# Moving the making of the Hyena filters from the second mixer to the end of the first

## The chip, the cores and the metric

The kernel runs on one core of one Trainium2 chip. The metric is the device time of one execution in microseconds (us); a row gives the median of several runs, or the one execution that the profiler recorded. TensorE (PE) does matmuls and transposes, VectorE (DVE), ScalarE (ACT) and GpSimd (POOL) do the rest, and SyncE (SP) issues most DMAs. GpSimd issues the others from its own instruction stream.

## The reference

Two layers of a model over 128 context tokens and 512 latent tokens, of width 1024. Layer 0 has a mixer of scans (S5 and RG-LRU), layer 1 a mixer with a long convolution (Hyena); after each mixer comes a layer of product-key experts (PEER).

```
def mixer_c(h, P, lo, grid):                       # layer 1
    z = h @ P['w_in_c'][lo] + P['b_in_c'][lo]      # 1024 -> 3 x 1024
    z = dwconv_rows(z, ...)
    x0, x1, v = split(z, 3)
    v = v * x1
    circ = hyena_filters(length, P['hy_w1'][lo], ..., P['hy_decay'][lo])
    v = bidir_long_conv(v, circ) + P['hy_bias'][lo] * v
    return (v * x0) @ P['w_out_c'][lo] + P['b_out_c'][lo]

def hyena_filters(length, w1, b1, f1, w2, b2, f2, w3, decay):
    z = sin(f1 * (emb @ w1 + b1))                  # positions only
    z = sin(f2 * (z @ w2 + b2))
    filt = (z @ w3).reshape(length, 2, HY_WIDTH)
    filt = filt * (exp(-t * abs(decay)) + HY_SHIFT)
    circ = concatenate([filt[:, 0], 0, filt[:0:-1, 1]])
    return circ * rsqrt(sum(circ * circ) + EPS)
```

What matters here: the filters hang on weights and positions alone, not on the activations. They can be made at any time before the long convolution of layer 1.

## The kernel before

All activations lie transposed (features on the 128 partitions, 640 tokens along them). The program runs four stages in turn: the first mixer (0 to about 452 us of the profile), the expert layer of layer 0, the second mixer (its input projections begin at about 2080 us), the expert layer of layer 1.

**Projections.** `proj3` (L164) multiplies one 128-column block of weights at a time. Each weight tile `wraw` comes by a DMA on SP into a ring of three buffers, ScalarE rounds it to `wh` (L159), GpSimd subtracts to get the rest `wl` (L77), and TensorE multiplies in three passes (L171): for a depth of 1024 that is 8 x 3 x 2 = 48 matmuls of 320 columns into `pproj`, for a depth of 512 it is 24. After each block `proj3` calls the function `evac` that it was given.

**The end of the first mixer.** `w_glu` gives 4 blocks of 24 matmuls, each followed by `evg` (a sigmoid on ScalarE, a product and a split on VectorE, into `mH`, `mL`). `w_out_ab` gives 8 blocks of 48 matmuls, each followed by `evo` (the addition to the residual stream `xT`, and its square for the next norm). Then `rms_rstd` sums the squares (`pssq`, L207) and broadcasts the norm by a matmul, `prs` (L225). The expert layer starts with that norm (`nt`, `hHg`, `hHd`), its transposes `phr`, and the query projections with `wq`.

**The second mixer's input projections.** `w_in_c` gives 24 blocks of 48 matmuls, each followed by `evc` (bias, a short convolution `zc` to `zo` on VectorE, and for every second block a product `vv` and five transposes `pva`, `pvb`). Then the convolution starts with a load of the kernel table `K`.

**The filters.** `filters(fp)` (L315) is a generator: each `next` issues one step, 43 in all.

- Two steps make the small network on 640 positions (matmul `pz`, reduction of the angle on VectorE, sine on ScalarE), into `zfin`.
- Then four chunks of 256 channels follow. A chunk loads `w3` and `dec` on SP, and does one small step for the context and four big steps for the latent tokens (k = 0 to 3). Each step is an exponential `f` (L350), the matmul `pf` (L353), their product (L95), a sum and a difference `pmf` (L77), a rounding to `pmpH`, `pmmH` (L360), subtractions to `pmpL`, `pmmL` on GpSimd, and a square; from the second big step on GpSimd adds the square to `sqa`.
- The chunk's tables are transformed with Fourier matrices `fc`, which GpSimd loads (L307, two buffers): six matmuls `pkf` for the context (L380), 48 for the latent tokens (L394). The results go to memory as `kf_dc` and `kf_ds` on SP. The sums of squares are reduced by `pss` (L372).
- The tiles `f`, `dec`, `sqa` and the four `PM` tiles have one buffer each, and `kfc`, the context's result, shares the tag and so the buffer of `f`:

```
                    kf = fp.tile([128, 2, CW], F32, name="kfc", tag="f", bufs=FBUF)
                    S.copy(kf, p)
                    nc.sync.dma_start(kf_d[0][:, :, c0:c0 + CW], kf)
```

Before the change, `mixer_c` takes FG0 = 6 steps ahead of the projections and FG1 = 3 in each `evc`, so all are issued by the 13th of the 24 blocks.

**What sets the order.** The code is written as a stream, but a scheduler places every instruction: it runs the program on a timeline of its own and puts on each engine whichever instruction is ready there. The order of each engine's instructions is then fixed, and an engine waits for the operand of its next instruction even when a later one could run. A tile waits for the readers of whatever lay in its memory before.

Of the kernel before, what the change touches and what calls it, by code (L numbers as in the profile page):

```python
# [43 lines left out]
def tile_kernel(ctx: ExitStack, tc: tile.TileContext, I, O, dbg=None, upto=99):  # L44
# [34 lines left out]
    def mul(o, a, b, eng=None):  # L79
        tt(o, a, b, ALU.mult, eng)  # L80

    def add(o, a, b, eng=None):
        tt(o, a, b, ALU.add, eng)
# [13 lines left out]
    def bc(a, shape):  # L97
        return a.to_broadcast(shape)
# [50 lines left out]
    def tick(n=1):  # L149
        for _ in range(n):  # L150
            if bgm[0] is None or next(bgm[0], False) is False:
                bgm[0] = None
                break
# [10 lines left out]
    def proj3(wsrc, nm, kk, segs, evac, pre=()):  # L164
        for m in range(nm):
            wh, wl = pre[m] if m < len(pre) else wsplit(wsrc[m])
            p = ps.tile([128, 2, 512], F32, name="pproj", tag="pp")
            for k in range(kk):
                for a, hl in ((wh, 0), (wh, 1), (wl, 0)):
                    for i, sg in enumerate(segs):  # L170
                        PE.matmul(p[:, i, :sg[2]], a[:, k, :], sg[hl](k), start=k == 0 and a is wh and hl == 0,  # L171
                                  stop=k == kk - 1 and a is wl)
            evac(m, p)

    def halves(H, L):
        def f(x, h):
            return lambda k: x[:, k, h * HALF:(h + 1) * HALF]
        return [(f(H, h), f(L, h), HALF) for h in range(2)]
# [23 lines left out]
    def rms_rstd(acc, pool, alloc, a=0, b=T, tag="", stag="sm"):  # L202
        n = (b - a) // 128
        p = ps.tile([128, 8], F32, name="pssq", tag=stag)
        add(acc[0], acc[0], acc[1])
        for i in range(n):
            PE.matmul(p[:, i:i + 1], acc[0][:, i * 128:(i + 1) * 128], ones[:, 0:1], start=True, stop=True)  # L207
        v, r, t = (pool.tile([128, 5], F32, name="nv" + c, tag="nv" + c + (tag or ""), bufs=1)[:, :n] for c in "abc")
        ts(v, p[:, :n], 1.0 / D, EPS, ALU.mult, ALU.add)
        S.activation(t, v, AF.Sqrt)  # L210
        V.reciprocal(r, t)
        mul(t, r, r)
        mul(t, t, v)
        ts(t, t, -0.5, 1.5, ALU.mult, ALU.add)
        mul(r, r, t)
        dg = alloc()[:, :b - a].rearrange("p (i c) -> p i c", c=128)
        sh = [128, n, 128]
        mul(dg, bc(ident.unsqueeze(1), sh), bc(r.unsqueeze(2), sh))
        if tag == "c":
            o = ps.tile([128, 512], F32, name="prs", tag="sm2")  # L220
        else:
            o = ps.tile([128, 2, 512], F32, name="prs", tag="pp").rearrange("p a b -> p (a b)")
        for i in range(0, n, 4):
            e = min(i + 4, n)
            PE.matmul(o[:, i * 128:e * 128], ones, dg[:, i:e].rearrange("p a b -> p (a b)"), start=True, stop=True)  # L225
        return o[:, :b - a]
# [44 lines left out]
    def resid(l, which, m, p):  # L271
        g = modT[l][:, which * 24 + 16 + m, :]
        for s, a, b in SEG:
            for h in range(2):
                lo, hi = max(a, h * HALF), min(b, (h + 1) * HALF)
                if lo < hi:
                    stt(xT[:, m, lo:hi], p[:, h, lo - h * HALF:hi - h * HALF], g[:, s:s + 1], xT[:, m, lo:hi],
                        ALU.mult, ALU.add)
# [30 lines left out]

    PASSES = ((0, 0), (0, 1), (1, 0))  # L310

    FBUF = 1
    PBUF = 2

    def filters(fp):  # L315
# [19 lines left out]
        for cc in range(D // CW):  # L335
# [8 lines left out]
            for sq_, ln, nk, tg in SEQS:  # L344
                PM = [[fp.tile([128, nk, CW], F32R, name=t, tag=t) for t in r] for r in PMT]
                sqa = fp.tile([128, 2, CW], F32, name="sqa", tag="sqa")
                for k in range(nk):
                    i = sq_ + k
                    f = fp.tile([128, 2, CW], F32, name="f", tag="f", bufs=FBUF)
                    S.activation(f, dec, AF.Exp, scale=tneg[:, i:i + 1])  # L350
# [24 lines left out]
                if sq_ == 0:  # L375
                    fc = fload(fp, "fc", I["fc_c"], 4)
                    p = ps.tile([128, 2, CW], F32, name="pkf", tag="sm2")
                    for ri in range(2):
                        for a, b in PASSES:
                            PE.matmul(p[:, ri], fc[:, ri * 2 + a], PM[ri][b][:, 0], start=(a, b) == (0, 0), stop=a == 1)  # L380
                    kf = fp.tile([128, 2, CW], F32, name="kfc", tag="f", bufs=FBUF)
                    S.copy(kf, p)
# [500 lines left out]
    with ExitStack() as ed:  # L883
        dp = ed.enter_context(tc.tile_pool(name="mxd", bufs=1))
        mH = dp.tile([128, 8, T], F32R, name="mH")
        mL = dp.tile([128, 8, T], F32R, name="mL")
        zH = dp.tile([128, 4, T], F32R, name="zH")
        zL = dp.tile([128, 4, T], F32R, name="zL")
        bg = vec("s5_b_glu")
        for j in range(4):  # L890
            split(zH[:, j], zL[:, j], zs[:, j])
            split(mH[:, 4 + j], mL[:, 4 + j], xg[:, j])

        tick(1000)

        def evg(m, p):
            t = dp.tile([128, T], F32, name="sg", tag="sg", bufs=2)
            S.activation(hv(t), pv(p), AF.Sigmoid, bias=bg[:, m:m + 1])
            mul(t, t, zs[:, m])
            split(mH[:, m], mL[:, m], t)  # L900

        proj3(I["w_glu"], 4, 4, halves(zH, zL), evg)
        def evo(m, p):
            resid(0, 0, m, p)
            one(m)

        acc, one = squares(lambda: dp.tile([128, T], F32, name="nsq", tag="nsq", bufs=6))
        proj3(I["w_out_ab"], 8, 8, halves(mH, mL), evo)
        rn[0] = rms_rstd(acc, dp, lambda: dp.tile([128, T], F32, name="nsq", tag="nsq", bufs=6))
    mx.close()  # L910
    dump("x1", xT)
# [10 lines left out]
    c_d = [dram.tile([ND, 128, 4, 2, 128], BF16, name=f"c_d{l}") for l in range(2)]  # L922
    g_d = [dram.tile([16, 128, TD // 16, 8, 16], F32, name=f"g_d{l}") for l in range(2)]

    FG0, FG1 = 6, 3
    ORD = (1, 2, 3, 4, 0)
    NGB = 5
    NGS = 3
# [482 lines left out]
    def mixer_c():  # L1411
# [4 lines left out]
        vH = mp.tile([128, 5, D], F32R, name="vH", tag="vmH")  # L1416
        vL = mp.tile([128, 5, D], F32R, name="vL", tag="vmL")
        bi, cw, cb = vec("b_in_c"), vec("hy_conv_w", 3, 24), vec("hy_conv_b")
        with ExitStack() as e0:
            ap, hH, hL = hc  # L1420
            fg = filters(e0.enter_context(tc.tile_pool(name="hyf", bufs=1)))
            order = [m for j in range(8) for m in (8 + j, 16 + j)] + list(range(8))
            pre = [wsplit(I["w_in_c"][m]) for m in order[:WPRE]]
            for _ in range(FG0):
                next(fg, None)
            x1 = [None]

            def evc(i, p):
                for _ in range(FG1):
                    next(fg, None)  # L1430
                m = order[i]
                z = ap.tile([128, T], F32, name="zc", tag="nrm", bufs=4)
                S.activation(hv(z), pv(p), AF.Identity, bias=bi[:, m:m + 1])
                o = ap.tile([128, T], F32, name="zo", tag="nrm", bufs=4)
                S.activation(o, z, AF.Identity, scale=cw[:, 1, m:m + 1], bias=cb[:, m:m + 1])
                ro, ri = (a.rearrange("p (r c) -> p r c", c=64) for a in (o, z))
                w0, w2 = cw[:, 0, m:m + 1], cw[:, 2, m:m + 1]
                stt(ro[:, :, 1:], ri[:, :, :63], w0, ro[:, :, 1:], ALU.mult, ALU.add)
                stt(ro[:, :, :63], ri[:, :, 1:], w2, ro[:, :, :63], ALU.mult, ALU.add)
                stt(o[:, 64:65], z[:, 63:64], w0, o[:, 64:65], ALU.mult, ALU.add)  # L1440
                stt(o[:, 63:64], z[:, 64:65], w2, o[:, 63:64], ALU.mult, ALU.add)
                if m < 8:
                    nc.sync.dma_start(x0_d[m], o)
                elif m < 16:
                    x1[0] = o
                else:
                    j = m - 16
                    mul(vv[:, j], o, x1[0], G)
                    pa = ps.tile([128, 4, 128], F32, name="pva", tag="sm")
                    pb = ps.tile([128, 4, 128], F32, name="pvb", tag="sm2")  # L1450
                    for i_ in range(5):
                        if i_ == 0:
                            tk = slice(0, TC)
                        else:
                            e, k = divmod(i_ - 1, 2)
                            tk = slice(TC + e + k * 256, TC + (k + 1) * 256, 2)
                        PE.transpose(pa[:, i_] if i_ < 4 else pb[:, 0], vv[:, j, tk], ident)
                    js = slice(j * 128, (j + 1) * 128)
                    S.copy(vH[:, 0:4, js], pa)
                    S.copy(vH[:, 4, js], pb[:, 0])  # L1460
                    sub(vL[:, 0:4, js], pa, vH[:, 0:4, js].bitcast(F32))
                    sub(vL[:, 4, js], pb[:, 0], vH[:, 4, js].bitcast(F32))

            proj3([I["w_in_c"][m] for m in order], 24, 8, halves(hH, hL), evc, pre)
            for _ in fg:
                pass
            e_c.close()
            bgm[0] = mods_ring(1, tuple(range(MQ, 10)))
        with ExitStack() as e1:
# [276 lines left out]
```

## Time and profile before

| | |
|---|---|
| median of 3 runs | 4136.21 us (4134.04 to 4140.57) |
| the profiled execution, its own time | 4135.69 us |
| its span, first to last instruction | 4133.9 us |
| mean granted TensorE clock, share of full speed | 0.938 |
| busy share of the span: PE, DVE, ACT, POOL | 87%, 82%, 40%, 55% |
| first mixer's gates and output projections | 373.1 to 452.2 us |
| second mixer's input projections, with the filters | 2079.8 to 2320.8 us |

Busy shares are averages over stages with different limits; a change is read from the stage that it touches. The chain that ended last is followed back from the last instruction to what released each step. The granted clock is a share of 2.4 GHz: 0.50 is 1.2 GHz, and values between are means over a stretch.

### The profile page before, as it was taken

The numbers are of one execution on the slowest core, as the hardware profiler recorded it, in microseconds if no ns is written. First come the engines' busy times: TensorE is split into PE (matmuls) and PEld (weight loads), VectorE is DVE, ScalarE is ACT, GpSimd is POOL, SyncE is SP. The second block draws the span as 40 slices with busy tenths as digits, with TensorE's granted clock in tenths as the row PEclk, the third lists the DMA queues.
The fourth block names the chain that finished last, engine by engine and source line by source line (L and its number), as shares of the span: only waits on it lengthen the run. The fifth ranks groups of instructions, "written<-read, shape, count | busy, mean of one in ns | idle before, by whom it ended". The sixth has DMA issues, their size and how long they took to land.

```text
span 4133.9 us, 57311 instructions
## 1 busy us (share of the span) xinstructions
PE 3603.9 (87%) x20066; PEld 3161.6 (76%) x20098; DVE 3370.1 (82%) x6122; ACT 1651.3 (40%) x3493; POOL 2273.9 (55%) x2046
## 2 busy tenths in 40 slices
PE   6867886598999999999689988843989999999996
PEld 4756874477899999999589778732778999999996
DVE  8873599899888887888865656998899888878889
ACT  3523333573333333333345334334733333333333
POOL 5641587668544444455655435886675444444455
PEclk9978997799999999999799999976999999999998
DMA  5565267498999999999724642653989999999997
GB/s 206 139 126 155 87 209 240 120 314 289 355 348 331 343 340 336 343 329 340 237 88 134 213 130 85 209 170 103 298 286 352 346 330 344 335 344 335 334 340 265
DMA packets 438105, 1057.42 MB, mean 256 GB/s; under 512 B 49175, under 2 KB 210967, under 8 KB 432696
## 3 DMA queue, kind: packets, MB, share of 16 engines
q0 software_dynamic: 152784, 555.55, 38.9%
q1 hardware_dynamic: 285032, 498.21, 35.4%
q8 instruction: 158, 2.59, 0.3%
q14 instruction: 131, 1.07, 0.1%
HBM read 993.86 MB, written 61.87 MB: 255 GB/s over the span
## 4 chain that ended last, share of the span: by engine, by line
PE 62%; DVE 23%; DMA 5%; issue 4%; POOL 3%; ACT 3%; SPq 1%; DVEq 0%; ACTq 0%; POOLq 0%
PE pA L1145 24%; PE pso L1295 23%; PE pproj L171 7%; DVE gb L1053 6%; PE pg L1245 2%; PE pmod L129 2%; DMA gb<-in_peer_u,ei 1%; DVE oh L77 1%; DVE OI L1240 1%; DMA mw<-in_w_mod 1%; POOL gb L1041 1%; DVE tiu L977 1%; DVE sc L978 1%; DVE tiu L980 1%; POOL jk L77 1%
## 5 line engine op out<-in xcount | busy, mean ns | idle before, releaser
L1041 POOL DMA_INDIRECT gb<-in_peer_v,ei x512 | 680.2, 1329 | 624.3 <-DVE acc L95 548.7
L1041 POOL DMA_INDIRECT gb<-in_peer_u,ei x512 | 637.7, 1245 | 529.8 <-DVE gb L1053 401.3
L1295 PE MATMUL pso<-vh,wp 128*128 128x512 f32 x3072 | 873.7, 393 | 3.7 <-ACT wp L1284 2.6
L1145 PE MATMUL pA<-hHd,ul 128*128 128x384 f32 x2048 | 691.5, 338 | 28.6 <-DVE ul L77 28.6
L1053 DVE SCALAR_TENSOR_TENSOR gb<-gb,hrow 128x1024 f32<-128x1024 f32 x512 | 701.9, 1378 | 16.4 <-DMA gb<-in_peer_u,ei 16.3
L1145 PE MATMUL pA<-hHd,uh 128*128 128x384 f32 x2048 | 692.8, 338 | 14.4 <-DVE modT L77 7.2
L1145 PE MATMUL pA<-hLd,uh 128*128 128x384 f32 x2048 | 690.9, 337 | 0.0
L95 DVE SCALAR_TENSOR_TENSOR acc<-gb,pw,acc 128x1024 f32<-128x1024 f32 x508 | 660.2, 1300 | 22.1 <-DMA gb<-in_peer_v,ei 18.7
L1295 PEld LDWEIGHTS pso<-vh,wp 128*128 128x128 f32 x3072 | 574.6, 188 | 112.6 <-ACT wp L1284 3.8
L1137 ACT CAST uh<-wraw 128x1024 fp32r<-128x1024 f32 x256 | 269.0, 1051 | 661.9 <-PE pA L1145 661.9
L77 DVE TENSOR_TENSOR ul<-wraw,uh 128x1024 fp32r<-128x1024 f32 x256 | 318.5, 1244 | 210.9 <-ACT uh L1137 208.6
L1295 PE MATMUL pso<-vl,wp 128*128 128x512 f32 x1536 | 479.4, 393 | 10.8 <-DVE vl L77 10.7
L1145 PEld LDWEIGHTS pA<-hHd,ul 128*128 128x128 f32 x2048 | 387.9, 189 | 31.6 <-DVE ul L77 30.3
L1145 PEld LDWEIGHTS pA<-hHd,uh 128*128 128x128 f32 x2048 | 388.3, 190 | 26.3 <-DVE modT L77 7.3
L1145 PEld LDWEIGHTS pA<-hLd,uh 128*128 128x128 f32 x2048 | 388.1, 189 | 8.8
L77 DVE TENSOR_TENSOR vl<-vraw,vh 128x1024 fp32r<-128x1024 f32 x256 | 314.1, 1227 | 63.8 <-ACT vh L1268 63.6
L1268 ACT CAST vh<-vraw 128x1024 fp32r<-128x1024 f32 x256 | 268.9, 1052 | 239.8 <-PE pso L1295 237.0
L1295 PEld LDWEIGHTS pso<-vl,wp 128*128 128x128 f32 x1536 | 289.2, 189 | 77.3 <-DVE vl L77 13.1
L77 POOL TENSOR_TENSOR wl<-wraw,wh 128x1024 fp32r<-128x1024 f32 (+1 forms) x88 | 215.4, 2449 | 229.4 <-ACT wh L159 206.5
L1284 ACT CAST wp<-A 128x384 fp32r<-128x384 f32 x256 | 131.5, 514 | 435.9 <-DVE A L77 410.3
L1245 PEld LDWEIGHTS pg<-OI,OJ 128*128 128x128 f32 x1536 | 204.2, 202 | 82.3 <-POOL OI L77 31.9
L1245 PE MATMUL pg<-OI,OJ 128*128 128x128 f32 x1536 | 216.2, 290 | 38.2 <-DVE OI L1240 21.6
(531 smaller groups left out, 6670.3 us busy)
## 6 DMA issues: line engine op xcount, KB each, us to landing
wraw<-in_uT SPq DMA_DIRECT2D x256, 512.0 KB, 6.1
vraw<-in_peer_v SPq DMA_DIRECT2D x256, 512.0 KB, 6.5
g_d<-Gs SPq DMA_DIRECT2D x48, 768.0 KB, 6.8
Gt<-g_d SPq DMA_DIRECT2D x24, 1536.0 KB, 10.8
wmod<-in_w_mod SPq DMA_DIRECT2D x48, 512.0 KB, 5.6
wraw<-in_wq SPq DMA_DIRECT2D x32, 512.0 KB, 3.7
mw<-in_w_mod SPq DMA_DIRECT2D x16, 1024.0 KB, 10.9
wraw<-in_w_in_c SPq DMA_DIRECT2D x24, 512.0 KB, 4.3
```

The costliest lines, as they stand in the source:

```text
L77: (eng or V).tensor_tensor(o, a, b, op=op)
L95: V.scalar_tensor_tensor(o, a, s, b, op0=op0, op1=op1)
L129: PE.matmul(pm[:2, :cw], cond[:, k], w[k], start=k == 0, stop=k == 7)
L171: PE.matmul(p[:, i, :sg[2]], a[:, k, :], sg[hl](k), start=k == 0 and a is wh and hl == 0, stop=k == kk - 1 and a is wl)
L1041: G.indirect_dma_start(out=b, out_offset=None, in_=I[tab], in_offset=bass.IndirectOffsetOnAxis(ap=ei[:, s:s + 1], axis=0))
L1053: V.scalar_tensor_tensor(b, b, 1.0, hrow[:, i], op0=ALU.mult, op1=ALU.mult, accum_out=act[:, s:s + 1])
L1137: S.copy(uh, u)
L1145: PE.matmul(pA, a[:, k], b[:, k], start=k == 0 and b is hHd and a is uh, stop=k == 7 and a is ul)
L1245: PE.matmul(pg[:, t], OJ[:, t4 * 4 + t], OI[:, t4 * 4 + t], start=True, stop=True)
L1268: S.copy(vh, v)
L1284: S.copy(WH, A)
L1295: PE.matmul(pso[n][h], a[:, c], b[:, h * 512:(h + 1) * 512], start=i == 0 and a is WH and b is vh, stop=i == 127 and a is WL)
```

## The change

The generator is started at the end of the first mixer. Its pool `hyf` is opened beside `mxd`, six steps are issued after the last of the modulation matmuls (`tick(1000)`), three in each `evg` and each `evo`, and the rest after the last output projection, ahead of `rms_rstd`. That makes 6 + 12 x 3 = 42 of 43 steps in the stream by the last `evo`. In `mixer_c` all calls of the generator are taken out, and the pool with them. Nothing else is edited, and what the filters compute is the same.

```
+    FG0, FG1 = 6, 3
     FBUF = 1
...
         tick(1000)
+        fg = filters(ed.enter_context(tc.tile_pool(name="hyf", bufs=1)))
+        for _ in range(FG0):
+            next(fg, None)
 
         def evg(m, p):
+            for _ in range(FG1):
+                next(fg, None)
             t = dp.tile([128, T], F32, name="sg", tag="sg", bufs=2)
...
         def evo(m, p):
+            for _ in range(FG1):
+                next(fg, None)
             resid(0, 0, m, p)
             one(m)
...
         proj3(I["w_out_ab"], 8, 8, halves(mH, mL), evo)
+        for _ in fg:
+            pass
         rn[0] = rms_rstd(acc, dp, lambda: dp.tile([128, T], F32, name="nsq", tag="nsq", bufs=6))
...
-    FG0, FG1 = 6, 3
...
-        with ExitStack() as e0:
+        with nullcontext():
             ap, hH, hL = hc
-            fg = filters(e0.enter_context(tc.tile_pool(name="hyf", bufs=1)))
...
-            for _ in range(FG0):
-                next(fg, None)
...
             def evc(i, p):
-                for _ in range(FG1):
-                    next(fg, None)
...
-            for _ in fg:
-                pass
             e_c.close()
```

The scheduler decides where this puts them. Lines of the changed kernel are one to nine higher than before (`pkf` L394 is L395, `pf` L353 is L354, `phr` L1084 is L1093).

**TensorE at the end of the first mixer.** Before, the last output projections (`mH`, `mL` with `wh`, `wl`) are followed at once by the norm (`pssq`, `prs`), its transposes and the query projections:

```order
L171 MATMUL pproj<-mL,wh 128x320 x2
L171 MATMUL pproj<-mH,wl 128x320 x2
L207 MATMUL pssq<-ones,nsq 128x1 x5
L225 MATMUL prs<-nsq,ones 128x512
L225 MATMUL prs<-nsq,ones 128x128
L1084 MATMUL phr<-ident,nt 128x128 x4
L171 MATMUL pproj<-hHg,wh 128x256
```

With the change the last output matmul is followed by the third big step (`pf`) and the transforms (`pkf`) of the second chunk:

```order
L171 MATMUL pproj<-mH,wl 128x320 x2
L354 MATMUL pf<-w_3002,zfin 128x256 x2
L395 MATMUL pkf<-pmpH,fc 128x256
L395 MATMUL pkf<-pmmH,fc 128x256
L395 MATMUL pkf<-pmpL,fc 128x256
```

No projection follows until the fourth chunk's last transform is done, and the norm's broadcast `prs` stands behind that:

```order
L395 MATMUL pkf<-pmmL,fc 128x256
L395 MATMUL pkf<-pmmH,fc 128x256
L225 MATMUL prs<-nsq,ones 128x512
L225 MATMUL prs<-nsq,ones 128x128
L1093 MATMUL phr<-ident,nt 128x128 x4
L171 MATMUL pproj<-hHg,wh 128x256
```

So the norm and the query projections moved behind two and a half of the four chunks: 12 of the 20 `pf` steps stand between the last output projection and `prs`, and 8 stand among the gates and output projections.

**ScalarE at a chunk's small step.** Before, in the second mixer, the rounding, the copy `kfc` and the next exponentials `f` stand among the projections' work (`wh`, `zc`, `zo`, `vH`):

```order
L360 CAST pmpH<-pmf 128x256
L360 CAST pmmH<-pmf 128x256
L1460 CAST vH<-pvb 128x128
L159 CAST wh<-wraw 128x1024
L1433 ACTIVATE zc<-pproj,vecs 128x640
L1435 ACTIVATE zo<-zc,vecs 128x640
L382 COPY kfc<-pkf 128x512
L1460 CAST vH<-pvb 128x128
L350 ACTIVATE f<-dec,tneg 128x512
```

With the change, in the third and fourth chunks, they stand alone:

```order
L361 CAST pmpH<-pmf 128x256
L361 CAST pmmH<-pmf 128x256
L383 COPY kfc<-pkf 128x512
L351 ACTIVATE f<-dec,tneg 128x512
L364 ACTIVATE sqa<-f 128x512
```

The filters' own order is as before; the other work between its steps is gone.

**TensorE in the second mixer.** Before, transforms stand between the projections, here in the second chunk:

```order
L1457 MATMUL pva<-ident,vv 128x128 x4
L171 MATMUL pproj<-chL,wh 128x320
L171 MATMUL pproj<-chH,wl 128x320 x2
L394 MATMUL pkf<-pmpH,fc 128x256
L171 MATMUL pproj<-chH,wh 128x320
L394 MATMUL pkf<-pmmH,fc 128x256
```

With the change only projections and the transposes of `vv` are left there:

```order
L171 MATMUL pproj<-chH,wl 128x320 x2
L1461 MATMUL pva<-ident,vv 128x128 x4
L1461 MATMUL pvb<-ident,vv 128x128
L171 MATMUL pproj<-chH,wh 128x320 x2
L171 MATMUL pproj<-chL,wh 128x320 x2
```

All 216 `pkf`, and the `pf`, `pss` and `pz` with them, have left this stretch.

## Rows read from the trace of the kernel before

**Rows 1.** The page: the span, and the chain that ended last by engine.
```profile
span 4133.9 us, 57311 instructions
...
PE 62%; DVE 23%; DMA 5%; issue 4%; POOL 3%; ACT 3%; SPq 1%; DVEq 0%; ACTq 0%; POOLq 0%
```

**Rows 2.** Windows: length; PE, PEld, DVE, ACT, POOL busy (instructions); clock; DMA share, GB/s.
```profile
2079.80:2320.80 241.00, 237.34 (x1558) 222.61 (x1558) 140.94 (x246) 119.19 (x199) 128.62 (x109) 0.99 0.39 123
373.10:452.20 79.10, 74.89 (x480) 73.68 (x480) 28.27 (x40) 27.20 (x35) 28.83 (x14) 0.95 0.26 89
452.20:461.80 9.60, 2.30 (x10) 2.21 (x10) 5.76 (x12) 3.01 (x4) 2.34 (x1) 0.67 0.17 55
```

**Rows 3.** Groups on PE, 2079 to 2321 us: xcount, busy us, mean ns, idle before.
```profile
L171 PE MATMUL pproj<-chL,wh 128*128 128x320 f32 x384 | 91.8, 313 | 0.0
...
L353 PE MATMUL pf<-w,zfin 64*128 64x256 f32 x80 | 23.4, 406 | 0.3 <-DVE f L95 0.3
L394 PE MATMUL pkf<-pmmH,fc 128*128 128x256 f32 x64 | 15.9, 289 | 1.9 <-DMA fc<-in_fc_s 1.0 <-ACT pmmH L360 0.9
...
L372 PE MATMUL pss<-ones,sqa 128*128 128x1 f32 x64 | 7.6, 238 | 0.0
```

**Rows 4.** Chain that ended last, second mixer: start us, us, what, how many.
```profile
2146.41 0.78 PE pss L372 x8
...
2150.66 1.06 PE pf L353 x4
...
2152.35 2.88 PE pkf L394 x24
...
2214.47 8.80 PE pproj L171 x60
```

**Rows 5.** Groups on ACT, 2079 to 2321 us: the sine's table load.
```profile
L333 ACT ACT_TABLE_LOAD x1 | 1.3, 1283 | 0.0
```

**Rows 6.** Timeline of PE, first mixer: start, us, what [idle before, releaser].
```profile
397.25 0.81 PE L171 MATMUL pproj<-mH,wh 128*128 128x320 f32 x2 [2.33 <-ACT mH L268]
```

**Rows 7.** DMA issues by line: xcount, KB each, median us to landing.
```profile
fc<-in_fc_s POOLq DMA_DIRECT2D x24, 512.0 KB, 4.9
...
xT<-in_xT SPq DMA_DIRECT2D x2, 2560.0 KB, 20.2
```

**Rows 8.** Chain that ended last, first mixer's end.
```profile
397.25 54.91 PE pproj L171 x362
...
461.84 2.49 PE prs L225 x4
```

**Rows 9.** Tiles f, pmf, kfc: xcount, ns min/median/max, first and last start; landing of kf_dc.
```profile
L77 DVE TENSOR_TENSOR pmf<-f x40: 406/424/2631, 2102.1 to 2289.3; 128x256 f32<-128x256 f32 x40
L350 ACT ACTIVATE f<-dec,tneg x20: 711/723/727, 2063.7 to 2287.1; 128x512 f32<-128x512 f32 x20
L95 DVE SCALAR_TENSOR_TENSOR f<-f,pf x20: 672/687/690, 2099.4 to 2287.9; 128x512 f32<-128x512 f32 x20
...
L77 POOL TENSOR_TENSOR sqa<-sqa,f x12: 1282/1292/1304, 2130.6 to 2292.3; 128x512 f32<-128x512 f32 x12
...
L360 ACT CAST pmpH<-pmf x20: 387/405/410, 2102.6 to 2289.4; 128x256 fp32r<-128x256 f32 x20
...
L77 POOL TENSOR_TENSOR pmpL<-pmf,pmpH x20: 720/742/1207, 2103.1 to 2289.8; 128x256 fp32r<-128x256 f32 x20
...
L382 ACT COPY kfc<-pkf x4: 575/585/587, 2110.7 to 2267.2; 128x512 f32<-128x512 f32 x4
...
DMA to landing us min/median/max: 2.6/4.3/5.6
```

**Rows 10.** Chain that ended last, second chunk: two exponentials in turn.
```profile
2168.67 0.73 ACT f L350
...
2171.70 0.73 ACT f L350
```

**Rows 11.** Window ahead of the second mixer's projections, columns as in Rows 2.
```profile
2060.00:2070.00 10.00, 2.29 (x4) 1.12 (x4) 8.35 (x18) 7.58 (x11) 3.65 (x3) 0.50 0.03 8
```

## The prediction

> **What bounds the kernel now.** I read the page first: the run is mostly a TensorE chain, which holds 62% of the chain that ended last [rows 1]. So the change is read in the two stretches it touches, by windows. In the second mixer's input projections, 2079.8 to 2320.8 us, TensorE is busy 237.3 of 241.0 us at clock 0.99, and VectorE 140.9 [rows 2]. At the first mixer's end, 373.1 to 452.2, TensorE is busy 74.9 of 79.1, VectorE 28.3, ScalarE 27.2 [rows 2]: those two are mostly free there, TensorE is not. In both, more matmuls mean more time. The chain of waits then shows what the second stretch hides: the filters run beside 24 projections of 48 matmuls, and their own waits (a small table's write, sums of squares, table loads) lie under projections.
>
> The reader is to see two things. First, filter matmuls cost TensorE about the same in either place. Second, the filters are also a long serial chain, and the first mixer has only 12 projections (4 of 24 matmuls, 8 of 48) where the second has 24 of 48. The question is what of the chain is left when the 12 are done.
>
> **What is given back in the second mixer.** The projections alone are 3 x 384 = 1152 matmuls [rows 3]; 60 of them take 8.80 us [rows 4], so 1152 take 169.0. The filter matmuls that leave: 80 pf records at 1.06 us for 4, 21.2 us; 216 pkf (192 large, and by the code 24 small) at 2.88 for 24, 25.9; 64 pss at 0.78 for 8, 6.2 [rows 3, 4]; the two layers of the small network some 2. That is 55 us, the lower bound. The upper one: 241.0 - 169.0 = 72, less some 5 for 40 transposes that stay, is 67; the 12 between are stalls on filter matmuls standing in order, and a slow start, of which I take rather more than half. **Gain 62 us (55 to 67).** Nothing else comes up there: without the filters VectorE, ScalarE and GpSimd have less to do than now, and the rows say that TensorE bounds. The wait for the kernel table K behind the last store stays.
>
> **What is added up to the last output projection.** The order of the changed kernel puts 8 of the 20 filter steps, the first chunk's transforms and the second's small one between the projections: 8 x 1.06 = 8.5, 60 pkf x 0.12 = 7.2, 3 pss x 0.78 = 2.3, the network 2.5. **20.5 us** at full clock.
> - Waits at the front: ScalarE must now switch tables among the four sigmoids. It gets three more table loads of 1.28 us [rows 5] and an absolute value, an exponential and a sine (0.7 each): 5.9 us on an engine for which TensorE already waits 2.3 us before the output projections [rows 6]. The network's inputs are also queued on SP behind the 2.5 MB reload of xT, which takes 20.2 us to land [rows 7]. Bounds 0 (all beside the gates) and 14 (that load lands in full first). I take 6, the ScalarE work alone.
> - Stalls in order: the 12 us of the second mixer are for four chunks; two chunks, 6 us (0 to 12).
>
> So the last output projection ends at 452.2 [rows 8] + 20.5 + 6 + 6 = 484.7.
>
> **What is left after it.** In the order, the last output matmul is followed by the second chunk's later steps, then chunks three and four whole, and only then by prs, the matmul that broadcasts the next layer's norm. Before, prs starts at 461.84 [rows 8], 9.6 us after the last projection, and nothing stands between. Now a serial chain does. One chunk, from the last subtraction of one to that of the next, with single buffers f, PM and dec:
> 1. The last sum of squares, 1.29 us on GpSimd [rows 9], stands before the issue of the next two transform tables, which land 4.9 us after issue [rows 7]: 6.2.
> 2. Their 24 matmuls, 2.9, with one pss (0.8) and one pf (1.1) between: 4.8.
> 3. The next chunk's small step may now write PM: difference, cast and two subtractions on GpSimd (0.42, 0.41, 0.74 twice) [rows 9], some 2.9 with waits.
> 4. Its six matmuls, 0.7, and the copy kfc, 0.6 [rows 9].
> 5. kfc has the tag of f, with one buffer, so the next exponential waits for its write to memory: 4.3 us median [rows 9].
> 6. Four big steps. From the first exponential to the second 3.0 us (2168.67 to 2171.70) [rows 10]. The next two need the GpSimd sum as well: 0.72 + 0.69 + 0.42 + 0.41 + 2 x 0.74 + 1.29 = 5.0 [rows 9], 5.2 with gaps, so 10.4. The last to its second subtraction, 3.7.
>
> Sum 6.2 + 4.8 + 2.9 + 1.3 + 4.3 + 17.1 = 36.6 us at full clock. TensorE is busy for less than half of that, and where it is so idle now the granted clock is 0.50, that is 1.2 GHz (2060 to 2070 us, busy 2.3 of 10) [rows 11]; the 5.5 us of matmuls in steps 2 and 4 then take up to twice as long. **I take 41 us a chunk.** Bounds: 35, at full clock with the shortest write seen, 2.6 us [rows 9]; and 52.2, the spacing now, (2267.2 - 2110.7) / 3 between the kfc copies [rows 9], where projections stand in the way on every engine.
>
> At the last projection the second chunk's small transform has just ended: copy and write 4.8 us, big steps 17.1, so 21.9. Then 2 x 41 = 82. Then the last tables and transforms at the slow clock, 6.2 + 5.8 = 12. Together 115.9 us, against 9.6 before: **106.3 us lost.** TensorE has nothing else: the query projections need the norm, and its tiles lie where the filters' do. The kernel's writes kf_ds and the load of the keys come behind on SP, beside the norm; the cold start of the query projections exists now too (clock 0.67 in 452.2 to 461.8 [rows 2]). Both at nothing: without that cover one load, as the 4.9 us of [rows 7].
>
> **The sum.** 20.5 + 6 + 6 + 106.3 - 62 = +76.8 us. The profiled execution took 4135.7 us (its span is 4133.9 [rows 1]), 0.5 below the median 4136.2, so 4212.5, said as 4212.
>
> The Trainium skill speaks to the table loads: DMA: Bandwidth & Descriptors, section Anatomy of one DMA, fits a descriptor queue's transfer as about 2.0 us plus its bytes at 436 GB/s. For 512 KB that is an estimate of 3.2 us where the row has 4.9, and three waits of 1.7 us less would give 4207; the row is from this kernel, with other loads in flight, and the sum goes by it.
>
> **The rivals.**
> - *The chain is at its floor.* Queues are idle after the projections, so loads and writes land fast and the clock stays up: 35 us a chunk, no waits at the front: -12 - 6 - 5, about 4189. For it: the tail has nearly no other transfers. Against: two engines' gaps per step do not shrink.
> - *The chain keeps its pace of now.* 52 us a chunk, +22, and front waits of 14, +8: 4242. For it: the slow clock doubles every filter matmul, and the order was laid out for other durations. Against: the projections' casts, splits and convolutions, which stretch it now, are gone.
> - *TensorE work is only moved.* If TensorE alone sets both stretches, what is given back is what is added, and the time is 4136. For it: 75 of 79 us busy. Against: only 8 of 20 steps stand between projections. The Trainium skill's Perfetto Trace Analysis, Identifying the Most-Contended Engine, would have it so: optimize the engine with the highest occupancy first. By that rule alone the change is worth nothing, and the trace agrees as long as the engine is busy, not once a chain leaves it idle.
> - *Faster: the rest of the chain runs beside the next stage.* The place is the norm and the first query projections. If the broadcast prs did not stand behind the last transforms, the tail would cost nothing, and the change 32.5 - 62 = -29.5: 4106. The point from which it decides: less than 62 - 32.5 + 9.6 = 39 us between the last projection and prs. That asks (39 - 34) / 2 = 2.5 us a chunk, or prs ahead in TensorE's order. For it: the chain needs little of any engine. Against: the order has prs last, and four big steps alone are 17 us.
>
> **How the numbers follow.** Forecast 0.70, floor 0.12, pace of now 0.13, work moved 0.02, faster 0.03. The first three are one mechanism at three paces. Their bounds: chunks -12 to +22, front -6 to +8, stalls -6 to +6, gain 62 -7 to +5; not all fall to one side at once, so -30 to +34: 4182 to 4246. That leaves out the last two cases and the far ends of the others, under 2 in 10. A measurement of this kernel can tell some 0.2%, 8 us, from no change. Slower by more: 0.95; within: 0.02; faster: 0.03.
>
> **What would show it right or wrong.** Right: the chain after the last output projection (about 485 us) runs through exponentials, sums, kfc's write and table loads for about 116 us, with TensorE busy under half and its clock near 0.5; prs starts near 600; kfc copies there are some 41 us apart; the second mixer's projections take about 179 us in place of 241, dense. Wrong: prs within 40 us of the last projection (then faster); copies 52 us apart (the high end); the second stretch over 190 us, bound by something other than filter matmuls.

## The result, and the profile after

| | before | changed |
|---|---|---|
| median of 4 runs | 4135.76 us (4134.04 to 4140.57) | 4202.07 us (4198.40 to 4206.82) |
| ratio to before, 95% interval | 1 | 1.0157 (1.0145 to 1.0170) |
| span of the profiled execution | 4133.9 us | 4196.6 us |
| mean granted clock | 0.938 | 0.927 |

Slower by 66 us in the medians and by 62.7 in the two profiled spans. The windows of the changed kernel, with the columns of [rows 2], show where:

```profile
374.50:475.30 100.80, 96.94 (x604) 88.87 (x604) 49.07 (x86) 48.75 (x73) 46.71 (x37) 0.98 0.40 125
475.30:584.00 108.70, 70.30 (x250) 53.91 (x251) 37.44 (x91) 36.87 (x76) 39.60 (x50) 0.58 0.35 102
...
2208.10:2383.80 175.70, 175.70 (x1193) 175.65 (x1194) 67.94 (x120) 69.20 (x91) 69.38 (x39) 0.99 0.26 83
```

The first line is the gates and output projections: 100.8 us in place of 79.1 [rows 2], and TensorE has 22.0 us more to do in them, so all of the growth is work. The second line is new. For 109 us after the last output projection no engine but TensorE is busy for more than 40 us, and TensorE's 70 are counted at a granted clock of 0.58, between 1.2 GHz (0.50) and 2.4, where it waits between short bursts; in the dense stretches of the first and third lines it is 0.98 and 0.99. The third is the second mixer's projections, 175.7 us in place of 241.0, with no gap on TensorE and the other engines at half of what they had.

The chain of waits of the changed kernel, in order of time (start, us, what), shows one turn of the chain in that stretch, and its end:

```profile
474.52 4.88 DMA kf_dc<-kfc
479.49 0.73 ACT f L351
480.24 0.70 DVE f L95
482.96 0.63 ACT f L351
...
488.04 0.73 ACT f L351
...
493.13 0.73 ACT f L351
...
496.93 1.28 POOL sqa L77
498.25 1.87 PE pss L373 x8
500.12 2.00 PE pf L354 x4
502.12 2.86 PE pkf L395 x12
...
507.10 1.64 PE pkf L395 x12
...
513.31 5.00 DMA kf_dc<-kfc
...
579.74 4.99 PE pkf L395 x24
...
586.60 4.39 DMA wraw<-in_wq
591.20 2.30 ACT nt L260 x4
```

The write of `kfc` holds the first exponential, the four exponentials follow at 3.5, 5.1 and 5.1 us, the last sum of squares releases `pss`, and the transforms run at first at the low clock: 12 `pkf` take 2.86 us, later 1.64. No load of a table `fc` stands in this turn: two are issued at 498.13, as the sum ends, and `pss` and `pf` fill the 3.9 us between the sum and the first transform. The copies `kfc`, from ScalarE's timeline, give the length of a turn:

```profile
422.96 0.59 ACT L383 COPY kfc<-pkf 128x512 f32<-128x512 f32 x1 [7.19 <-PE pkf L381]
473.91 0.59 ACT L383 COPY kfc<-pkf 128x512 f32<-128x512 f32 x1 [4.24 <-PE pkf L381]
512.70 0.59 ACT L383 COPY kfc<-pkf 128x512 f32<-128x512 f32 x1 [1.61 <-PE pkf L381]
551.00 0.59 ACT L383 COPY kfc<-pkf 128x512 f32<-128x512 f32 x1 [1.81 <-PE pkf L381]
```

It is 51.0 us beside projections and 38.8 and 38.3 without them. TensorE's timeline shows its longest wait in a turn, and the norm's broadcast, which stood at 461.84 before [rows 8]:

```profile
519.98 2.04 PE L354 MATMUL pf<-w,zfin 64*128 64x256 f32 x4 [7.37 <-DVE f L95]
...
584.55 1.24 PE L225 MATMUL prs<-nsq,ones 128*128 128x512 f32 x4
```

In the second mixer the chain is projections and transposes alone, and behind them the load of K as before:

```profile
2208.07 25.83 PE pproj L171 x162
...
2234.49 14.08 PE pproj L171 x96
...
2387.73 4.49 DMA x_d<-zo
2392.30 8.63 DMA K<-kf_ds
```

From these and the starts of the first query projection (468.4 us before, 593.7 now) the 62.7 us are found whole:

| stretch | forecast | measured |
|---|---|---|
| start of the gates | 0 | +1.4 |
| to the last output projection | +32.5 | +21.7 |
| from there to `prs`, against 9.6 before | +106.3 | +99.6 |
| `prs` to the first query projection (6.6 before, 9.2 now) | 0 | +2.6 |
| to the second mixer's first projection (1611.4, 1614.4) | 0 | +3.0 |
| second mixer's projections | -62 | -65.3 |
| the rest | 0 | -0.3 |
| sum | +76.8 | +62.7 |

### The profile page after: what moved, and what is told of

Its sections match the earlier page's. It is cut to its first block, busy times and chain, and to the rows that moved or that the text cites. A ratio compares the mean times of both kernels' runs of the same rounds, so it can differ in the third digit from the quotient of the medians.

```text
span 4196.6 us, 57367 instructions
## 1 busy us (share of the span) xinstructions
PE 3636.9 (87%) x20098; PEld 3186.8 (76%) x20098; DVE 3347.2 (80%) x6122; ACT 1656.3 (39%) x3492; POOL 2259.7 (54%) x2046
## 4 chain that ended last, share of the span: by engine, by line
PE 61%; DVE 24%; DMA 5%; issue 4%; POOL 3%; ACT 3%; SPq 1%; DVEq 0%; ACTq 0%; POOLq 0%
PE pA L1154 23%; PE pso L1304 23%; PE pproj L171 8%; DVE gb L1062 6%; PE pg L1254 2%; DMA gb<-in_peer_u,ei 1%; PE pmod L129 1%; DVE oh L77 1%; DVE OI L1249 1%; DVE gt L77 1%; DVE tiu L986 1%; DVE tiu L989 1%; DVE sc L987 1%; DMA gb<-in_peer_v,ei 1%; DVE ef L1027 1%
```

## The experiments

The theory: the filters are one serial chain; under projections it costs TensorE its matmuls, without them its full length. The rival throughout: TensorE's own matmuls, and the clock that they get, set the cost in both places.

**1. Two buffers for f and kfc, in the changed kernel.**

```
-    FBUF = 1
+    FBUF = 2
```

> The changed kernel (4202 us) with FBUF = 2: two buffers for f and kfc; the matmuls and everything else are the same. Theory, serial chain: the tail after the last output projection is a row of waits of which the single buffer makes a part. With two buffers the write of kfc (5.0 us from issue to landing) no longer holds back the next exponential, and the exponential of a step runs beside the subtractions of the step before. Expected 38.5 us between kfc copies in the tail down to 27 to 33, two and a half chunks of it: 15 to 28 us less, 4174 to 4187 us. Rival, TensorE's own matmuls at the slow clock set the tail: their number is the same, so no change, 4198 to 4206 us.

Measured: 4171.8 us, 30 less, with the same matmuls, and just below the range expected. The copies:

```profile
507.57 0.59 ACT L383 COPY kfc<-pkf 128x512 f32<-128x512 f32 x1 [1.69 <-PE pkf L381]
541.99 0.59 ACT L383 COPY kfc<-pkf 128x512 f32<-128x512 f32 x1 [1.70 <-PE pkf L381]
```

A turn is 34.4 us, not the 27 to 33 expected: the write still stood on the chain of this run, and a load came up beside it:

```profile
508.18 4.99 DMA kf_dc<-kfc
...
524.53 4.06 DMA fc<-in_fc_s
```

Up to the first query projection the profiled execution gains 16 us; another 9 lie in the expert layer (1605.2 us in place of 1614.4), where nothing was edited. This part is not explained. So 16 us are shown to be the buffers': a change of buffers alone takes off a quarter of the 62.7 us, and that part of the loss is waits, not matmuls. TensorE isn't far behind the chain, though. From the last output projection to `prs` it is counted busy for 74.2 of 91.6 us in this run, at a clock of 0.53 (70.3 of 108.7 in the changed kernel). How much shorter the chain could get before TensorE at that clock sets the time was not tried.

**2 and 3. Two chunks in place of four, in the changed kernel and in the one before.** Half of the filter computation is left out in both.

```
-        for cc in range(D // CW):
+        for cc in range(2):
...
-                    nc.sync.dma_start(kf_d[1][ft, :, :, c0:c0 + CW], kf)
+                    for c2 in (c0, c0 + 2 * CW):
+                        nc.sync.dma_start(kf_d[1][ft, :, :, c2:c2 + CW], kf)
```

> The changed kernel with only two of the four chunks made (half of the filter computation is left out; each chunk's results are written to two column ranges). Theory, serial chain: the two chunks that go are wholly in the uncovered tail, 38.3 to 38.8 us each, so 77 us less: 4125 us (4118 to 4132), and prs starts about 24 us after the last output projection. Rival, TensorE's own matmuls set the cost: two chunks are 27 us of matmuls at full clock, up to 45 at the slow clock: 4157 to 4175 us.

> The kernel before (4136 us) with only two of the four chunks made (half of the filter computation is left out). Theory: in the second mixer a chunk costs its matmuls, 13.7 us at full clock, and some 2 us of stalls: two chunks fewer give 28 to 33 us, 4103 to 4108 us. Rival: the 65 us that the second mixer gave back are mostly the waits of the chain and its slow start, not matmuls; those sit in the first chunk, and two later chunks fewer give 15 us or less: 4121 us or more.

Measured: 4123.1 and 4106.9 us, that is 79 and 28 us less than the four chunks cost in each kernel. This pair is the plainest reading: the same two chunks cost 79 us behind the last projection and 28 under projections. In the second mixer the projections took 208.5 us with two chunks; with four they took 241.0 and with none 175.7, so 16.3 us a chunk, evenly. In the changed kernel with two chunks, `prs` began 30 us after the last output projection, 6 later than expected.

**4. The norm ahead of the filters in TensorE's order.**

```
-        rn[0] = rms_rstd(acc, dp, lambda: dp.tile(...))
+        rn[0] = rms_rstd(acc, dp, lambda: dp.tile(...), stag="pp")
```

> The changed kernel with the sum of squares pssq in the PSUM tag of the projections instead of the tag of the filters, so that the norm no longer follows the last filter step in that tag's rotation; the scheduler then puts pssq right behind the last output projection and prs two chunks earlier. Theory, memory: the tiles of the query stage lie where the filters' tiles lie and its transposes share the filters' PSUM tag, so the first query projection still waits for the end of the chain: 0 to 9 us less (the norm's own time), 4193 to 4202 us. Rival, the order of prs alone keeps the next stage behind the filters: the query projections start 60 to 90 us earlier, 4112 to 4142 us.

Measured: 4210.0 us, 8 more. TensorE's timeline of this run:

```profile
491.65 2.47 PE L225 MATMUL prs<-nsq,ones 128*128 128x512 f32 x4
...
602.01 0.47 PE L1093 MATMUL phr<-ident,nt 128*128 128x128 f32 x1 [6.54 <-ACT nt L260]
...
603.94 0.56 PE L171 MATMUL pproj<-hHg,wh 128*128 128x256 f32 x1
```

The broadcast comes 93 us earlier, and the first product `nt` that uses it still starts at 600.5, after the last transform. So the order of `prs` is not what kept the next stage behind the filters. VectorE's timeline shows the last wait ahead of `nt`:

```profile
600.33 0.24 DVE L95 SCALAR_TENSOR_TENSOR gm<-modT,vecs 128x8 f32<-128x8 f32 x2 [3.61 <-DMA kf_ds<-kf]
```

`gm` reads only `modT` and `vecs`, and yet VectorE waits for the write of the filters' last result `kf_ds` to land. That points to the memory of the tiles, as the theory had it. Whether the shared PSUM tag or the order on VectorE alone would still hold the stage wasn't told apart. The turns grew to 45.1 and 41.5 us. In the first of them the norm's own work stands (`prs` itself is at 491.65); why the second grew isn't settled.

**5 and 6. A tile of its own for kfc, f still single; then also the first two tables ahead of the third big step.**

```
-                    kf = fp.tile([128, 2, CW], F32, name="kfc", tag="f", bufs=FBUF)
+                    kf = fp.tile([128, 2, CW], F32, name="kfc", tag="kfc")
...
+                    if k == 2:
+                        early = [fload(fp, "fc", I["fc_s"][0, ri], 8) for ri in range(2)]
...
-                        fc = fload(fp, "fc", I["fc_s"][ft, ri], 8)
+                        fc = early[ri] if ft == 0 else fload(fp, "fc", I["fc_s"][ft, ri], 8)
```

> The changed kernel (4202 us) with a tile of its own for kfc, and f still with one buffer: only the wait of the next exponential for the write of kfc goes. Theory, the write is one serial term of the chain: a chunk in the tail gets shorter by the write's 5.0 us and the 0.1 around it, the copies of kfc 33.5 us apart in place of 38.5; three writes stand on the chain after the last output projection, so 12 to 16 us less, 4186 to 4190 us. Rival, the write only covers another wait that takes its place (as with two buffers of f, where a write and table loads both stood on the chain): 0 to 6 us less, 4196 to 4202 us.

> The kernel of the run before (own tile for kfc) with the first two tables fc_s of a chunk issued before its third big step in place of after the last. Theory: the load's wait behind the last sum of squares, forecast at 6.2 us a chunk with the sum, now lies under two steps of 5.1 us; a chunk gets shorter by another 2 to 5 us (in the profile of the changed kernel the sum, pss and pf already cover most of the 4.9 us of the load), 28.5 to 31.5 us; over two and a half chunks 5 to 13 us less than the run before. Rival: the table load is hidden under pss and pf at the slow clock anyway: no more than 2 us less than the run before.

Measured: 4182.2 us, 20 less than the changed kernel, and 4182.6 with the early tables. The write is a serial term: `prs` comes 85 us after the last output projection, in place of 109. It was worth more than expected, since the second chunk, still under projections, came earlier too:

```profile
418.11 0.59 ACT L383 COPY kfc<-pkf 128x512 f32<-128x512 f32 x1 [0.78 <-PE pkf L381]
456.82 0.58 ACT L383 COPY kfc<-pkf 128x512 f32<-128x512 f32 x1
499.94 0.58 ACT L383 COPY kfc<-pkf 128x512 f32<-128x512 f32 x1 [1.13 <-PE pkf L381]
534.16 0.58 ACT L383 COPY kfc<-pkf 128x512 f32<-128x512 f32 x1 [1.13 <-PE pkf L381]
```

From the first copy to the fourth it is 116.1 us in place of 128.0. From the start of the gates to the first query projection the profiled execution gains 21 us, more than the 16 of experiment 1. The medians have it the other way round (20 and 30), since the expert layer behind, which neither edit touches, took 1622.8 us here and 1605.2 there.

The early tables tested nothing. GpSimd's timelines, of experiment 5 and then of experiment 6, have the same issues behind the last sum of squares:

```profile
515.60 1.26 POOL L77 TENSOR_TENSOR sqa<-sqa,f 128x512 f32<-128x512 f32 x1
516.81 1.09 POOL L307 DMA_DIRECT2D fc<-in_fc_s  x2
...
519.50 1.27 POOL L77 TENSOR_TENSOR sqa<-sqa,f 128x512 f32<-128x512 f32 x1
520.71 1.09 POOL L307 DMA_DIRECT2D fc<-in_fc_s  x2
```

A chunk has four tables `fc_s`, and the first two, which the edit names, were issued ahead of the big steps without it (in the changed kernel at 509.03 and 512.91). The two behind the sum are the second pair. So the equal times say nothing on what that load costs.

**7. Only the first chunk moved.** `filters` is given its chunks, `range(0, 1)` in the first mixer and `range(1, 4)` in the second, where the calls that the change took out are put back.

> Only the first chunk is made at the end of the first mixer, the other three beside the second mixer's input projections as before (the small network is made in both places). In the order all of the chunk's matmuls stand ahead of the last output projection. Theory: where the chain has projections to lie under, moving costs nothing: 13.7 us of matmuls, 2.5 of the network and 0 to 3 of stalls are added in the first mixer, one chunk's 16.2 us (half of the 32.5 that two chunks took in the second mixer) is given back: 0 to +3 us, with the scatter of the expert layer 4130 to 4146 us against 4136 before. Rival, each chunk costs the same wherever in the first mixer's end it is made, a quarter of the 66 us: 4152 us.

Measured: 4140.0 us, ratio 1.0010 (1.0001 to 1.0018): 4 us more, not 16. Its windows, columns as in [rows 2]:

```profile
374.40:472.10 97.70, 94.79 (x578) 87.51 (x578) 48.67 (x85) 46.98 (x69) 43.65 (x32) 0.94 0.35 112
2104.30:2330.40 226.10, 222.84 (x1468) 211.72 (x1468) 127.15 (x219) 108.33 (x173) 113.48 (x91) 0.99 0.35 113
```

The first mixer's end grows by 18.6 us and the second mixer's projections shrink by 14.9. A chunk that fits under the projections is moved at nearly no cost; the others pay for the lack of cover.

**8. Two buffers for f and kfc, in the kernel before** (the edit of experiment 1).

> The kernel before (4136 us) with FBUF = 2, so the filters' chain there gets the two buffers that took 30 us off the changed kernel. Theory: beside the projections the chain is hidden and TensorE bounds; of the 12 us that the second mixer takes beyond its matmuls some are stalls of this chain: 0 to 6 us less, 4130 to 4136 us. Rival, the chain bounds there as well: its chunk of 52 us shortens by as much as in the tail, 4 us each, 12 to 30 us less, 4106 to 4124 us.

Measured: 4129.6 us, ratio 0.9985 (0.9974 to 0.9996), 6 us less; faster than both kernels, if by little.

```profile
2082.00:2318.80 236.80, 236.35 (x1558) 222.72 (x1558) 136.05 (x246) 119.41 (x199) 132.08 (x109) 0.99 0.40 125
```

Its copies `kfc` run from 2113.2 to 2243.4, 43.4 us apart in place of the 52.2 of [rows 9], but of the 26 us by which this chain got shorter only the 3 to 4 us of gaps on TensorE came off the projections (3.7 idle of 241.0 before, 0.5 of 236.8 now). The same edit was worth 16 us of its stretch, and 30 in the medians, without cover.

**9 to 11. Cheaper matmuls pf in the kernel before.** If a covered chain costs its matmuls alone, shorter matmuls should show in full. (Of the products, the rest of the network times the rest of `w3` is left out.)

```
-                        PE.matmul(p[:, h], src[:, i * 128:(i + 1) * 128], w3[:, h], start=True, stop=True)
+                        PE.matmul(p[:, h], src[:, i * 128:(i + 1) * 128], w3H[:, h], start=True, stop=False)
+                        PE.matmul(p[:, h], src[:64, i * 128:(i + 1) * 128], w3L[:, h], start=False, stop=True)
```

> The kernel before (4136 us, filters beside the second mixer's projections) with each f32 matmul pf (two records, 0.53 us) replaced by two rounded ones: the positions' network stands twice on the partitions, its rounded half above and the rest below, against w3 rounded, and the upper half once more against the rest of w3. The same products but one that is small are formed. Theory, beside the projections a filter matmul costs its own TensorE time and nothing else: 80 records of pf, 21.2 us, become 80 matmuls of 256 columns at the 0.12 us of pkf, 9.6 us: 8 to 13 us less, 4123 to 4128 us, and the projections of the second mixer take about 230 us in place of 241. Rival, the stretch is set by the chain of the filters: the new loads and castings of w3 lengthen it, and the time stays or rises: 4133 to 4142 us.

> The kernel of the run before with FBUF = 2 and PBUF = 1 (memory has no room for both at two). Theory: the stalls that two buffers of f took away in the kernel before (6 us of the measured medians) come off here too, less what the single buffer of pmf gives back: 4118 to 4127 us. Rival: with one buffer of pmf each step's rounding and subtractions must end before the next difference, which stretches the chain until it is no longer covered: 4128 us or more.

> As the kernel with the short pf, but the raw w3 is loaded into its own tile again, so its load no longer waits for the sums of squares of the chunk before (there the kfc copies were 56 to 61 us apart in place of 52, the chain ended after the projections, and the table K was loaded 9 us later than before). The rest of w3 goes through the two pmf tiles, one more copy on ScalarE. Theory, a filter that ends under its cover costs its matmuls alone: the copies of kfc at most 53 us apart, the projections some 230 to 234 us in place of 241, and the end of the filters ahead of them: 6 to 12 us less than before, 4123 to 4130 us. Rival, even so the chain of the filters ends with or behind the shortened projections, and the load of K waits for it: 4131 to 4141 us.

Measured: 4141.3, 4154.0 and 4155.5 us, ratios 1.0010 (1.0000 to 1.0020), 1.0043 (1.0029 to 1.0058) and 1.0050 (1.0036 to 1.0064). All three expectations of the theory failed, and the rivals held in their mechanism, though the third run lies 14 us beyond its rival's range. With the new loads, castings and single buffers the chain got longer (its copies are 59, 62 and 63 us apart on average), and it ran out from under the projections. The projections end earlier in all three, after 234.7 us in the first and 226.2 in the last. But in the last run, from its ScalarE timeline, the fourth copy comes only 5 us before the projections end:

```profile
2241.81 0.58 ACT L398 COPY kfc<-pkf 128x512 f32<-128x512 f32 x1 [2.36 <-PE pkf L396]
2305.41 0.59 ACT L398 COPY kfc<-pkf 128x512 f32<-128x512 f32 x1
```

and its chain of waits has the rest of the filters bare, up to the load of K:

```profile
2322.03 0.73 ACT f L365
...
2332.12 4.62 DMA fc<-in_fc_s
2336.88 2.90 PE pkf L410 x12
...
2346.41 3.39 DMA kf_ds<-kf
2350.07 12.55 DMA K<-kf_ds
```

The first product with K starts 278.0 us after the first projection here; before it was 257.1, with two buffers of f 253.3, in the changed kernel 192.9. This is the loss of the change again, in the other mixer and by another edit. In the kernel before the last 24 `pkf` end 18 us ahead of the projections: that is about all the room that its chain had. Which of the added steps stretched a turn by 11 us in the last of the three isn't settled; in the second a load of `w3` of 6.84 us stands on the chain.

## Why the prediction was right, and where its sizes were off

Forecast +76.8 us, measured +66 in the medians, inside the range, by the mechanism that was named.

- **What bounds, and the question of cover.** Right. Experiments 2, 3 and 7 show it: a chunk costs some 14 to 19 us on either side where projections cover it, 38 to 40 where none do. The rival of work only moved fell. What stands for it in the trace, TensorE busy 75 of 79 us, was true up to the last output projection and ended there.
- **Gain in the second mixer, 62.** Measured 65.3; the upper bound was 67. Nearly all of the 12 us of stalls and slow start went with the matmuls. Nothing else came up, and the wait for K stayed, as said.
- **Added up to the last output projection, 20.5 + 6 + 6.** The matmuls were 22.0 us; the two other terms were nothing. This is the largest miss. TensorE's idle time in this stretch was 4.2 us before and 3.9 after. ScalarE did get its three table loads among the gates (at 388.60, 392.20 and 398.14 us), and a fourth at 428.60, but TensorE did not wait longer for it. The reload of xT held nothing up: the network's first matmul ran at 383.8, among the gates.
- **A turn of the chain, 41 us.** Measured 38.5. Step 6 held (exponentials 3.5, 5.1 and 5.1 us apart in the turn shown against 3.0 and 5.2), step 5 was 5.0 in place of 4.3. What was mis-sized is the 4.4 us put on top of 36.6 for the slow clock. Steps 1 and 2 were 11.0 at full clock, and the turn shown has 11.8 for them, from the last sum at 496.93 to the last transform at 508.74 (11.4 in the next turn). The sum put the load of the tables, 4.9, ahead of everything else. In the trace it runs beside `pss` and `pf`, which take 3.9 at the low clock and which the sum had left out at that place. So half of the slow clock's price (`pss` and `pf` 3.9 in place of 1.8) falls into time that was counted for the load. Of the transforms, the first 12 pay it (2.86 in place of 1.44) and the second 12 hardly (1.64). No run here moved that load.
- **The tail, 115.9 us.** Measured 109.2; `prs` began at 584.6 where "near 600" was said, and 9 of these 16 us are the front's. One sign of being right failed: TensorE was to be busy for under half of the stretch, and it is counted busy for 70.3 of 108.7 us, since its matmuls take longer at the low clock (four `pf` 2.00 in place of 1.06).
- **The cold norm, at nothing.** It cost 2.6 us: a load of `wq` of 4.39 us came onto the chain, near the 4.9 that were named as the price without cover.
- **The rival of the faster side** had two conditions. Experiment 4 met the second, `prs` ahead in TensorE's order, and the time rose: that condition was wrong as I put it. The chain is also far from the 39 us that the first asks, even with two buffers (92 us from the last projection to the end of the last transforms) or with a tile of its own for `kfc` (85).
- **Pages.** The Trainium skill, Perfetto Trace Analysis, section Roofline, says that a kernel with matmul and memory use both low is bound by latency. The bare tail agrees in part: its DMA share is 0.35 and TensorE waits up to 7.4 us in a turn, but TensorE is counted busy for 70.3 of 108.7 us. That waits set the time there is shown by experiments 1 and 5. The section that the prediction weighed, Identifying the Most-Contended Engine of the same page of the Trainium skill, says which engine to optimize first. That the change is worth nothing was a reading of it, and the runs decided against that reading.

## What to carry to other kernels

Before moving a side chain, set its length beside the length of the work that is to cover it, and count where it ends, not only what it costs the busy engine. Here the same two chunks cost 28 us under cover and 79 behind it, and in the old place the chain had 18 us of room, which an edit meant to make it cheaper used up. Buffers are worth most on a chain that lies bare (16 us of the stretch here, 30 in the medians) and little on one that is covered (4 and 6).

## What the runs showed of the hardware that was not expected

At the gates a switch of ScalarE's tables cost no more than the load. In the timeline of the changed kernel a sigmoid ends at 398.12 us, the load follows at 398.14 and takes 1.28:

```profile
397.33 0.79 ACT L904 ACTIVATE sg<-pproj,vecs 128x640 f32<-128x640 f32 x1
398.14 1.28 ACT L334 ACT_TABLE_LOAD   x1
399.43 0.74 ACT L334 ACTIVATE zpmpL<-zpmpL 64x640 f32<-64x640 f32 x1
```

The Trainium skill, ScalarE: Activation LUTs, section What ACT_TABLE_LOAD costs, adds a drain of about 1.38 us to each switch; no such gap stands at this one, nor at the load at 388.60, where a cast ends at 388.58 and the exponential starts at 389.89. The measurement decides here.

The expert layer of layer 0 took from 1605 to 1623 us in the profiled executions of kernels that differ only in other stages (1611.4 before, 1605.2 in experiment 1, 1622.8 in experiment 5). An edit changes the order that the scheduler gives to later stages, and single executions of one kernel differ as well (by 16 us in experiment 8). Which of the two it is was not tried. A difference of under some 18 us between two kernels can come from here, and is better read from the stretch that an edit touches.
